# Output projection of a hybrid decoder layer: operand loads on another queue, a buffer for the sum of two weight blocks, later splits and a store in pieces

## The chip, the cores and the metric

The kernel runs on one core of a Trainium2 chip. The time is device microseconds (us) of one execution; lower is better. A core has a matrix engine (TensorE, PE in the profile), a vector engine (VectorE, DVE), a scalar engine (ScalarE, ACT), GpSimd (POOL) and SyncE (SP). Transfers between device memory and the on-chip memory are issued by SP, ACT or POOL, each strictly in the order of its own queue, and moved by 16 DMA engines.

## The reference

One decoder layer over a prompt of 1024 tokens and 8 x 8 sample tokens, with model width 2048. RMSNorm and one input projection make five groups of 1024 columns; group A goes through a short convolution and a gated linear recurrence, group B through a gate, a convolution of width 31, LayerNorm and SiLU. Both halves, `ya` and `yb`, then go through one output projection, a residual sum and a final RMSNorm:

```
proj = jnp.einsum('btd,de->bte', xn, w_in)             # input projection, split in five
...
y = jnp.einsum('bte,ed->btd', jnp.concatenate([ya, yb], axis=-1), w_out)
return x32 + y, h[:, -1], new_buf_a, new_buf_b          # then the final RMSNorm over x32 + y
```

Everything is float32.

## The kernel before, in words

**Splits.** PE multiplies numbers of reduced mantissa (float32r). So every operand is split into a high part, a cast on ACT, and a low part, the operand minus its high part on DVE. A product of two operands is three matmuls: high x high, high x low, low x high.

**The input projection** takes the first 979 us. At its end `finish_b(i)` (L687) makes, for each of the eight blocks of channels, the operands of the output projection and stores them to device memory through POOL: `d7d`, `yd`, `o2d` (L698 to L702). It needs the A half `ya`, which `load_a(i)` (L665) loads through SP (L668); the tile `ya` has one buffer, so the load waits until the store of `o2d` of block i-1, which reads that buffer, has ended. For the last block `load_a(NC - 1)` and `finish_b(NC - 1)` are called behind the last projection.

**The output projection** is done in blocks, with seven products of half-size matrices in place of eight (the list `products`, L753 on). Each product p takes rows of one stored operand (`d6d`, `o2d`, `d7d`, `yd`) and either one block of `w_out` or the sum or difference of two; its result is added to one or two quarters of the output, which start as the residual `x`. Products 0 to 6 run in that order. A product has two column halves j of 512 and eight steps k in each, 16 steps in all; a step is four token tiles x three matmuls of 128 x 512 (L852 to L854), and in products 1, 3, 4 and 5 two more for the sample tokens (L860). After the eighth step of a half DVE adds the four banks of results to `c` (L983), so that the banks come free.

**Per step.** `load_w(s)` (L806) loads one or two 256 KB weight blocks through SP (L817) into `or`; `split_out(s)` (L828) adds the two in place on DVE (L843, products 0, 2, 3, 4 and 6), casts the high part on ACT (L844) and subtracts on DVE (L845). The tile `or` is free after L845. There are eight such tiles in products 0 and 1 (they lie where the input projection's operands lay) and five after that; the split is called two steps ahead of the matmuls (`AHEAD`), and its high and low parts have three buffers.

**Operands.** `load_op(p, k)` (L771) loads one 256 KB operand block through SP (L776) and splits it at once (L777 on ACT, L778 on DVE). It is called for product p+1 at step 2k of product p; its tile is the one that step k of product p-1 used. The eight loads of product 0 are called ahead of its first step.

**Queues.** The order of instructions on an engine is the order of a planner: it simulates the engines' clocks and gives each engine, at each moment, the ready instruction of the best priority. Priority is the program's order; `tc.high_priority(URGENT)` moves instructions 200 places ahead, `tc.high_priority(-LATER)` 400 back. So an instruction can be put ahead of its place in the program where the planner finds it ready. On the chip each engine then follows that order strictly.

**The end.** The last eight steps are done one token tile at a time. For each of the four tiles the row scale comes out of `inverse` (L873), ACT scales 768 columns (L1013), DVE 1024 and 256 (L1014, L1016), and two stores of 512 KB go out on SP (L1015, L1017).

Of the kernel before, what the change touches and what calls it, by code (L numbers as in the profile page):

```python
# [7 lines left out]
F32 = mybir.dt.float32  # L8
F32R = mybir.dt.float32r
AF = mybir.ActivationFunctionType  # L10
ALU = mybir.AluOpType
# [3 lines left out]
P = 128  # L15
# [3 lines left out]
NC = W // P  # L19
# [4 lines left out]
T = SEQ + NS  # L24
# [11 lines left out]
URGENT = 200  # L36
LATER = 400
# [26 lines left out]
def hybrid_layer_kernel(  # L64
# [21 lines left out]
    nc = tc.nc  # L86
    V, S, G, PE = nc.vector, nc.scalar, nc.gpsimd, nc.tensor
# [3 lines left out]
    wp = ctx.enter_context(tc.tile_pool(name="wp", bufs=3))  # L91
# [147 lines left out]
    yd = [dp.tile([P, T], F32, name=f"yd{k}") for k in range(NK)]  # L239
# [6 lines left out]
    AHEAD = 2  # L246
# [12 lines left out]
    NH = NK // 2  # L259
# [144 lines left out]
    def tt(name, dt=F32):  # L404
        return kb.tile([P, 364], dt, tag="t", name=name, bufs=9)
# [259 lines left out]
    def load_a(i):  # L665

        ya = early[i] = kb.tile([P, AS + DB * AW], F32, tag="xa", name=f"ya{i}")
        nc.sync.dma_start(ya[:, :T], yd[i])  # L668
        if i == NC - 1:
            return  # L670
        h = G0 // 2
        for o in (0, h):
            d = tt(f"d6_{i}_{o}")[:, :h]
            V.tensor_sub(d, ya[:, G0 + o : G0 + o + h], ya[:, o : o + h])
            G.dma_start(d6d[i][:, o : o + h], d)
# [28 lines left out]
    for n in range(4 * NC, 5 * NC):  # L704
        i = n - 4 * NC
# [31 lines left out]
    H = D // 2  # L737
    NB = H // 512
    NN = G0 // P
    NH = NK // 2  # L740

    def rows(tiles, o):
        return lambda k: tiles[k][:, o : o + G0]

    def smp(tiles, o):
# [6 lines left out]
    products = [  # L752
        (rows(d6d, 0), ((0, 0), add, (0, 1)), (((1, 1), add),), None),  # L753
        (rows(o2d, 0), ((0, 0), None, None), (((1, 0), add), ((1, 1), sub)), s12),
        (rows(d7d, G0), ((0, 0), add, (1, 1)), (((0, 0), add), ((1, 1), add)), None),
        (rows(b_y, G0), ((1, 0), sub, (0, 0)), (((0, 0), add), ((1, 0), add)), s2),
        (rows(a_y, 0), ((0, 1), sub, (1, 1)), (((0, 1), add), ((1, 1), add)), s1),
        (rows(b_y, 0), ((1, 1), None, None), (((0, 0), sub), ((0, 1), add)), s12),
        (rows(d7d, 0), ((1, 0), add, (1, 1)), (((0, 0), add),), None),
    ]  # L760
# [8 lines left out]
    cq, ops, sops, osplit = {}, {}, {}, {}  # L769

    def load_op(p, k):  # L771
        b = p % 2 * NH + k
        hi = xp.tile([P, G0], F32R, tag=f"h{b}", name=f"yh{p}_{k}")
        lo = xp.tile([P, G0], F32R, tag=f"l{b}", name=f"yl{p}_{k}")
        raw = lo.bitcast(F32)
        nc.sync.dma_start(raw, products[p][0](k))  # L776
        S.copy(hi, raw)  # L777
        V.tensor_sub(lo, raw, hi.bitcast(F32))  # L778
        ops[p, k] = (hi, lo)

    def load_samples(src, name):

# [37 lines left out]
    def load_ahead(s):  # L820

        while (t := len(begun)) < last0 and t < s + (NH if steps[t][0] < 2 else 5):
            load_w(t)
            begun.append(t)
# [3 lines left out]
    def split_out(s):  # L828
        if s not in wraw:
            load_w(s)  # L830
        p, j, k = steps[s]
        _, op, wb = products[p][1]
        ra, rb = wraw.pop(s)
        if s >= last0:

            big = xp.tile([P, H], F32R, tag=held[s - last0], name=f"ow{s}")
            hi, lo = big[:, :512], big[:, 512:]
        else:
            hi = wp.tile([P, 512], F32R, tag="wh", name=f"oh{s}")
            lo = wp.tile([P, 512], F32R, tag="wl", name=f"ol{s}")  # L840
        with tc.high_priority(URGENT):
            if wb is not None:
                V.tensor_tensor(ra, ra, rb, op)  # L843
            S.copy(hi, ra)  # L844
            V.tensor_sub(lo, ra, hi.bitcast(F32))  # L845
        osplit[s] = (hi, lo)
# [83 lines left out]
    def then(p, st, f):  # L930
        between.setdefault(p * NB * NH + st, []).append(f)

    for p in range(NP - 1):
        for k in range(NH):
            then(p, 2 * k, lambda p=p, k=k: load_op(p + 1, k))
        if products[p + 1][3] is not None:
            then(p, 4, lambda p=p: load_samples(*products[p + 1][3]))

# [16 lines left out]
    for k in range(NH):  # L955
        then(5, 9 + 2 * k, lambda k=k: split_out(last0 + k))

    for k in range(NH):
        load_op(0, k)
        load_ahead(k + 1 - NH)  # L960
    for s in range(AHEAD):
        split_out(s)
    for s, (p, j, k) in enumerate(steps[:last0]):
        _, _, dests, sm = products[p]
        if k == 0:
            pts = [bank(f"po{p}_{j}_{n}") for n in range(NN + (sm is not None))]
        load_ahead(s)
        if s + AHEAD < last0:
            split_out(s + AHEAD)
        for f in between.pop(s, ()):  # L970
            f()
        for n in range(NN):
            multiply(s, n, pts[n])
        if sm is not None:
            multiply_samples(s, pts[NN])
        osplit.pop(s)
        if k < NH - 1:
            continue
        js = slice(j * 512, (j + 1) * 512)
        with tc.high_priority(URGENT):  # L980
            for n in range(NN):
                for q, op in dests:
                    V.tensor_tensor(cq[q, n][:, js], cq[q, n][:, js], pts[n], op)  # L983
        if sm is not None:
            h = shalf[p]
            z = zs[0][:NS, h * H + j * 512 : h * H + (j + 1) * 512]

            low = ob.tile([P, 512], F32, tag="sq", name=f"zl{p}_{j}", bufs=2)[:NS]
            S.copy(low, pts[NN][NS:])
            V.tensor_tensor(z, z, pts[NN][:NS], ALU.add)  # L990
            V.tensor_tensor(z, z, low, ALU.add)
        if p == NP - 1:
            for n in range(NN):
                squares_of(n * P, P, cq[(0, 0), n][:, js], 2)
                gain(cq[(0, 0), n][:, js], 0)

    for n in range(NN):
        t = n * P
        z = cq[(0, 0), n]
        widths = ((0, 512),) if n < NN - 1 else ((0, 256), (256, 256))  # L1000
        for m, (c0, cn) in enumerate(widths):
            pt = bank(f"pz{n}_{m}")
            for k in range(NH):
                multiply(last0 + k, n, pt[:, :cn], slice(c0, c0 + cn))
            zz = z[:, 512 + c0 : 512 + c0 + cn]
            V.tensor_tensor(zz, zz, pt[:, :cn], ALU.add)
            squares_of(t, P, zz, 3 + m)
            if m < len(widths) - 1:
                gain(zz, 512 + c0)
        w = inverse(t, P, 3 + len(widths), lambda: gain(zz, 512 + c0))  # L1010
        zr = cq[(0, 1), n]
        h = 256
        S.activation(zr[:, h:], zr[:, h:], AF.Copy, scale=w)  # L1013
        V.tensor_scalar(z, z, w, None, ALU.mult)  # L1014
        nc.sync.dma_start(y[t : t + P, :H], z)  # L1015
        V.tensor_scalar(zr[:, :h], zr[:, :h], w, None, ALU.mult)  # L1016
        nc.sync.dma_start(y[t : t + P, H:], zr)  # L1017


# [76 lines left out]
```

## Time and profile before

| | us |
|---|---|
| median of 3 runs | 1351.22 (1349.5 to 1356.63) |
| profiled execution, its own time | 1354.75 |
| its span | 1353.0 |
| PE busy in it | 1321.1 (98%) |
| DVE busy | 1065.5 (79%) |
| ACT busy | 551.4 (41%) |
| POOL busy | 100.1 (7%) |

The profile is one execution, which took 3.5 us more than the median. A "busy" PE is a modelled figure, since matmuls overlap in the array; PE's real rate is read from how many matmuls a stretch holds. An idle time is shown with what ended it ("<-DVE c L983": an instruction of line 983 on DVE that wrote c). SPq, POOLq and so on are the queues that issue transfers.

### The profile page before, as it was taken

The page shows a single profiled execution, that of the slowest core. Times are in us where ns is not written, and L with a number is a line of the kernel's source. Part 1 is how long each engine was busy: PE and PEld are TensorE (multiplying, and loading weights), DVE is VectorE, ACT ScalarE, POOL GpSimd, SP SyncE. Part 2 cuts the span into 40 slices and gives each one's busy share as a digit, 9 for nine tenths or more (in the row PEclk, how much of TensorE's full clock was granted, in tenths as well). Part 3 has the DMA queues.
Part 4 walks back from the last instruction along what each step waited for, and adds up shares of the span by engine and source line. Part 5 has one row for each costly group of instructions (what it writes and reads, how often), then busy time and mean ns, then how long its engine had stood idle before and what let it go on. Part 6 is the DMA issues. An engine that isn't in the chain of part 4 may idle for free.

```text
span 1353.0 us, 18432 instructions
## 1 busy us (share of the span) xinstructions
PE 1321.1 (98%) x6794; PEld 1150.0 (85%) x6794; DVE 1065.5 (79%) x1842; ACT 551.4 (41%) x891; POOL 100.1 (7%) x190
## 2 busy tenths in 40 slices
PE   9999999999999999999999999999979999989997
PEld 7888888888888888888888898888868787768876
DVE  6449979898998996997987986766565676667977
ACT  7744627217237146155164165322232332224553
POOL 0210020100100010000001000012100000000100
PEclk9999999999999999999999999999989999999998
DMA  8831141312312322223123133276799668665663
GB/s 297 309 100 44 47 78 47 76 48 68 72 46 73 61 65 63 52 68 60 45 67 67 48 105 63 80 245 226 255 319 322 240 201 271 187 189 164 226 210 140
DMA packets 85946, 180.71 MB, mean 134 GB/s; under 512 B 14176, under 2 KB 18272, under 8 KB 85600
## 3 DMA queue, kind: packets, MB, share of 16 engines
q1 hardware_dynamic: 73952, 141.63, 34.0%
q0 software_dynamic: 11760, 37.90, 10.1%
q8 instruction: 53, 0.87, 0.3%
q14 instruction: 37, 0.30, 0.1%
q10 hardware_dynamic: 144, 0.01, 0.0%
HBM read 147.31 MB, written 32.19 MB: 133 GB/s over the span
## 4 chain that ended last, share of the span: by engine, by line
PE 74%; DMA 12%; DVE 10%; issue 1%; SPq 1%; ACT 0%; DVEq 0%; POOL 0%; ACTq 0%
PE pp L230 61%; DMA or<-in_w_out_dram 7%; DVE cb L449 4%; PE po L852 3%; PE po L854 3%; PE po L853 3%; PE po L860 1%; DVE ol L845 1%; DMA yl<-yd 1%; DVE c L983 1%; DMA yl<-o2d 1%; SPq L817 1%; DMA cbd<-cb 1%; DVE wl L160 1%; DMA c<-in_x_dram 1%
## 5 line engine op out<-in xcount | busy, mean ns | idle before, releaser
L230 PE MATMUL pp<-xg,wh 128*128 128x320 f32 (+1 forms) x1920 | 461.7, 335 | 1.2 <-DVE xg L194 1.2
L230 PEld LDWEIGHTS pp<-xg,wh 128*128 128x128 f32 x1920 | 320.3, 188 | 40.8 <-DVE xg L194 2.1
L449 DVE SCALAR_TENSOR_TENSOR cb<-u,prm,cb 128x1024 f32<-128x1024 f32 x240 | 307.2, 1280 | 1.3
L230 PE MATMUL pp<-xl,wh 128*128 128x512 f32 x640 | 250.9, 392 | 0.6 <-DVE xl L194 0.6
L230 PE MATMUL pp<-xh,wh 128*128 128x512 f32 x640 | 251.1, 393 | 0.4 <-ACT xh L193 0.3
L159 ACT CAST wh<-wr 128x512 fp32r<-128x512 f32 (+1 forms) x161 | 98.7, 614 | 341.7 <-PE pp L230 276.6
L230 PE MATMUL pp<-xg,wl 128*128 128x256 f32 (+1 forms) x1280 | 196.4, 296 | 0.0
L230 PEld LDWEIGHTS pp<-xg,wl 128*128 128x128 f32 x1280 | 186.0, 189 | 0.0
L852 PE MATMUL po<-oh,yh 128*128 128x512 f32 x416 | 165.7, 398 | 13.9 <-DVE c L983 7.6
L230 PE MATMUL pp<-xh,wl 128*128 128x512 f32 x640 | 171.2, 389 | 0.0
L853 PE MATMUL po<-ol,yh 128*128 128x512 f32 x416 | 165.5, 398 | 2.3 <-DVE ol L845 2.2
L854 PE MATMUL po<-oh,yl 128*128 128x512 f32 x416 | 164.8, 396 | 0.0
L160 DVE TENSOR_TENSOR wl<-wr,wh 128x512 fp32r<-128x512 f32 (+1 forms) x161 | 109.9, 683 | 46.4 <-ACT wh L159 29.4
L230 PEld LDWEIGHTS pp<-xh,wl 128*128 128x128 f32 x640 | 120.1, 188 | 25.0
L230 PEld LDWEIGHTS pp<-xh,wh 128*128 128x128 f32 x640 | 120.7, 189 | 21.5 <-ACT xh L193 0.9
L230 PEld LDWEIGHTS pp<-xl,wh 128*128 128x128 f32 x640 | 120.6, 189 | 20.6 <-DVE xl L194 1.5
L852 PEld LDWEIGHTS po<-oh,yh 128*128 128x128 f32 x416 | 79.9, 192 | 33.2 <-DVE c L983 9.3
L843 DVE TENSOR_TENSOR or<-or 128x512 f32<-128x512 f32 x80 | 54.2, 689 | 63.9 <-DMA or<-in_w_out_dram 63.4
L853 PEld LDWEIGHTS po<-ol,yh 128*128 128x128 f32 x416 | 79.9, 192 | 21.6 <-DVE ol L845 4.9
L844 ACT CAST oh<-or 128x512 fp32r<-128x512 f32 x104 | 64.1, 618 | 78.9 <-PE po L860 50.2
L854 PEld LDWEIGHTS po<-oh,yl 128*128 128x128 f32 x416 | 79.7, 192 | 16.7
L777 ACT CAST yh<-yl 128x512 fp32r<-128x512 f32 x56 | 34.7, 620 | 127.3 <-DMA yl<-yd 59.8
(218 smaller groups left out, 1409.4 us busy)
## 6 DMA issues: line engine op xcount, KB each, us to landing
or<-in_w_out_dram SPq DMA_DIRECT2D x192, 256.0 KB, 4.4
wr<-in_w_in_dram SPq DMA_DIRECT2D x152, 256.0 KB, 3.0
xt<-in_x_dram POOLq DMA_DIRECT2D x16, 512.0 KB, 6.4
c<-in_x_dram SPq DMA_DIRECT2D x16, 512.0 KB, 6.4
xraw<-in_xT_dram SPq DMA_DIRECT2D x15, 544.0 KB, 6.2
yl<-yd SPq DMA_DIRECT2D x24, 256.0 KB, 4.6
cbd<-cb POOLq DMA_DIRECT2D x8, 544.0 KB, 5.5
yd<-sga POOLq DMA_DIRECT2D x8, 544.0 KB, 8.8
```

Source lines behind the costliest of these rows:

```text
L159: S.copy(hi[:, sl], raw[:, sl])
L160: V.tensor_sub(lo[:, sl], raw[:, sl], hi[:, sl].bitcast(F32))
L230: PE.matmul(out, w, mv, start=fl, stop=ll)
L449: V.scalar_tensor_tensor(cb[:, :SEQ], u[:, j : j + SEQ], w, cb[:, :SEQ], ALU.mult, ALU.add)
L777: S.copy(hi, raw)
L817: nc.sync.dma_start(r, w_out[r0 : r0 + P, c0 : c0 + 512])
L843: V.tensor_tensor(ra, ra, rb, op)
L844: S.copy(hi, ra)
L845: V.tensor_sub(lo, ra, hi.bitcast(F32))
L852: PE.matmul(pt, yh, hi, start=k == 0, stop=False)
L853: PE.matmul(pt, yh, lo, start=False, stop=False)
L854: PE.matmul(pt, yl, hi, start=False, stop=k == NH - 1)
```

## The change

Four things change. (1) The sum of two weight blocks goes to a tile of its own, `ws`, with two buffers, and no longer in place. (2) The operand loads of all products but product 1 go through POOL's queue instead of SP's; from product 1 on they are called at step k, not 2k; the split is a function of its own, called five steps behind step 2k, and for product 0 two steps ahead of its matmuls, with URGENT priority. (3) The last `ya` load goes through POOL, with LATER priority. (4) Each of the last four token tiles is stored in four pieces: 384 KB on ACT's queue, two of 256 KB and one of 128 KB on SP's; DVE's scaling of 1024 columns is done in two halves.

```diff
     def load_a(i):
         ya = early[i] = kb.tile([P, AS + DB * AW], F32, tag="xa", name=f"ya{i}")
+        if i == NC - 1:
+            with tc.high_priority(-LATER):
+                G.dma_start(ya[:, :T], yd[i])
+            return
         nc.sync.dma_start(ya[:, :T], yd[i])
-        if i == NC - 1:
-            return
...
     def load_op(p, k):
         hi = xp.tile([P, G0], F32R, tag=f"h{b}", name=f"yh{p}_{k}")
         lo = xp.tile([P, G0], F32R, tag=f"l{b}", name=f"yl{p}_{k}")
+        (nc.sync if p == 1 else G).dma_start(lo.bitcast(F32), products[p][0](k))
+        ops[p, k] = (hi, lo)
+
+    def split_op(p, k):
+        hi, lo = ops[p, k]
         raw = lo.bitcast(F32)
-        nc.sync.dma_start(raw, products[p][0](k))
         S.copy(hi, raw)
         V.tensor_sub(lo, raw, hi.bitcast(F32))
-        ops[p, k] = (hi, lo)
...
     def split_out(s):
             if wb is not None:
-                V.tensor_tensor(ra, ra, rb, op)
+                ws = wp.tile([P, 512], F32, tag="wr", name=f"ws{s}", bufs=2)
+                V.tensor_tensor(ws, ra, rb, op)
+                ra = ws
             S.copy(hi, ra)
             V.tensor_sub(lo, ra, hi.bitcast(F32))
...
     for p in range(NP - 1):
         for k in range(NH):
-            then(p, 2 * k, lambda p=p, k=k: load_op(p + 1, k))
+            then(p, 2 * k if p == 0 else k, lambda p=p, k=k: load_op(p + 1, k))
+            then(p, 2 * k + 5, lambda p=p, k=k: split_op(p + 1, k))
...
+    def split_first(k):
+        with tc.high_priority(URGENT):
+            split_op(0, k)
+
+    for k in range(AHEAD, NH):
+        then(0, k - AHEAD, lambda k=k: split_first(k))
     for k in range(NH):
         load_op(0, k)
         load_ahead(k + 1 - NH)
     for s in range(AHEAD):
         split_out(s)
+        split_first(s)
...
         S.activation(zr[:, h:], zr[:, h:], AF.Copy, scale=w)
-        V.tensor_scalar(z, z, w, None, ALU.mult)
-        nc.sync.dma_start(y[t : t + P, :H], z)
+        nc.scalar.dma_start(y[t : t + P, H + h :], zr[:, h:])
+        for o in (0, 512):
+            V.tensor_scalar(z[:, o : o + 512], z[:, o : o + 512], w, None, ALU.mult)
+            nc.sync.dma_start(y[t : t + P, o : o + 512], z[:, o : o + 512])
         V.tensor_scalar(zr[:, :h], zr[:, :h], w, None, ALU.mult)
-        nc.sync.dma_start(y[t : t + P, H:], zr)
+        nc.sync.dma_start(y[t : t + P, H : H + h], zr[:, :h])
```

## Rows read from the trace of the kernel before

**Rows 1.** Stretches: length, busy us (instructions) per engine, PEclk, DMA share, GB/s.

```profile
979.00:1033.30 54.30, 46.99 (x194) 37.72 (x193) 35.44 (x58) 18.18 (x31) 1.59 (x3) 0.91 0.91 306
1033.30:1086.90 53.60, 51.52 (x225) 41.81 (x224) 32.18 (x53) 18.65 (x32) 0.00 (x0) 1.00 0.78 264
1086.90:1131.80 44.90, 44.18 (x194) 35.90 (x193) 33.16 (x54) 14.79 (x26) 0.00 (x0) 1.00 0.70 216
1131.80:1189.30 57.50, 54.14 (x225) 42.78 (x224) 36.81 (x59) 14.33 (x25) 1.08 (x4) 0.97 0.73 221
1189.30:1245.60 56.30, 53.02 (x226) 43.04 (x225) 37.90 (x62) 16.34 (x28) 0.00 (x0) 0.97 0.60 182
1245.60:1296.40 50.80, 50.80 (x226) 42.07 (x225) 40.64 (x81) 25.59 (x60) 4.27 (x8) 1.00 0.65 222
1296.40:1344.30 47.90, 45.87 (x217) 38.29 (x215) 41.44 (x89) 24.02 (x59) 0.54 (x1) 0.96 0.44 150
```

**Rows 2.** Timeline of PE: start, length, instruction, [idle before it <- what ended it].

```profile
990.80 0.80 PE L852 MATMUL po<-oh,yh 128*128 128x512 f32 x1 [6.12 <-ACT oh L844]
...
1194.59 0.50 PE L852 MATMUL po<-oh,yh 128*128 128x512 f32 x1 [3.04 <-DVE c L983]
```

**Rows 3.** Chain of waits, in order of time: start, length, what.

```profile
971.14 8.73 DMA o2d<-ya
...
1187.10 4.27 DMA yl<-yd
...
1191.39 0.63 ACT yh L777
...
1192.65 0.68 DVE ol L845
1193.34 2.40 DVE c L983 x4
...
1196.80 0.43 PE po L852
```

**Rows 4.** Waits of SP's queue from 960 us: us in total, times, longest.

```profile
SPq L817 <- DVE ol L845: 127.2, 69, 5.4
...
SPq L776 <- PE po L860: 23.1, 15, 3.2
SPq L668 <- DMA o2d<-ya: 9.0, 1, 9.0
```

**Rows 5.** Timeline of SP's queue from 1060 us.

```profile
1068.09 12.53 SPq L776 DMA_DIRECT2D yl<-yd  x5
```

**Rows 6.** Line 776, the operand loads: who waited for it (us, times).

```profile
  ACT yh L777: 126.1, 50
```

**Rows 7.** Waits in the output projection.

```profile
DVE or L843 <- DMA or<-in_w_out_dram: 63.4, 41, 5.2
```

**Rows 8.** Timeline of DVE in product 2.

```profile
1108.32 0.69 DVE L843 TENSOR_TENSOR or<-or 128x512 f32<-128x512 f32 x1 [1.51 <-DMA or<-in_w_out_dram]
1108.93 0.68 DVE L845 TENSOR_TENSOR ol<-or,oh 128x512 fp32r<-128x512 f32 x1
```

**Rows 9.** Groups of POOL: busy us, mean ns, idle before.

```profile
L453 POOL DMA_DIRECT2D cbd<-cb x8 | 4.4, 548 | 27.4 <-DVE cb L449 27.4
```

**Rows 10.** The page's transfers: count, KB each, median us from issue to landing.

```profile
or<-in_w_out_dram SPq DMA_DIRECT2D x192, 256.0 KB, 4.4
...
xt<-in_x_dram POOLq DMA_DIRECT2D x16, 512.0 KB, 6.4
...
yl<-yd SPq DMA_DIRECT2D x24, 256.0 KB, 4.6
...
yd<-sga POOLq DMA_DIRECT2D x8, 544.0 KB, 8.8
```

**Rows 11.** Timeline of all engines at the end.

```profile
1346.66 0.75 DVE L1014 TENSOR_SCALAR c<-c,r 128x1024 f32<-128x1024 f32 x1
...
1347.87 0.37 SPq L1017 DMA_DIRECT2D out_y_dram<-c  x1
```

## The prediction

> **What bounds the kernel now.** I read the stretches first, cut where the seven products of the output projection begin [rows 1]. A product is 16 steps of 12 matmuls (14 where the samples ride along). The product at 1245.6 us has 16 x 14 = 224 matmuls, PE busy all through, in 50.8 us: 0.2268 us each. By that pace a product of 192 takes 43.55 us, one of 224 takes 50.8, and the last stretch (168 full matmuls and 48 of half width) 43.55. Taken from the stretches this leaves a loss of 54.3-43.55 = 10.75, then 2.8, 1.35, 6.7, 5.5, 0 and 4.35 us: **31.4 us in which PE has work left and does not do it**. That is all the change can win before the last matmul; the tail has its own term below. The projection before 979 us is not touched.
>
> Next I looked at what ended PE's waits [rows 2]. The largest is 6.1 us before step 2 of the first product, ended by a cast of ACT; five others sit where a bank of results has to be emptied and DVE (L983) comes late; the one shown waited 3.0 us. After each large one matmuls run at 0.43 us for a while [rows 3], the lower clock level, which makes a stall dearer by about 2 us. Who made ACT and DVE late is in the chain of waits [rows 3]: a 256 KB operand load of 4.27 us, the cast that waits for it, the low half of a weight step behind that cast, and only then the four evacuations PE wants. ACT and DVE are late because they work strictly in their queue's order behind a transfer. Three couplings do this:
>
> (a) SP waits. 127.2 us go on `or` loads that wait for L845 to free a raw buffer, 23.1 on operand loads that wait for PE, and 9.0 once, on the last `ya`, behind the store of `o2d` [rows 4]. Five operand loads in a row, each released by a step of PE, held SP from 1068 to 1080.6 us, and the weight loads stood behind them [rows 5].
> (b) ACT waits 126.1 us in 50 casts for operand loads [rows 6]; `oh` stands behind them.
> (c) DVE waits 63.4 us in 41 adds for weight loads [rows 7]. The add of a later step stands ahead of an older step's L845 [rows 8], while the load it needs was issued after an L845 of two steps before. So two steps must cover a load (4.4 us [rows 10]), two issues and two DVE instructions: close to 6 us against 2 x 12 x 0.2268 = 5.4 us of PE work. The ring is five deep and acts as if it were two.
>
> **The change part by part.**
>
> The sum buffer adds no instruction and no memory traffic: the add writes elsewhere. In the two-block products the raw buffer is free after the add (0.69 us long [rows 8]) instead of after add, cast and subtraction; with two sum buffers an add can't run ahead of the subtraction two steps older. The ring then gives five steps, 13.6 us, to cover about 6 us. Coupling (c) should go in products 0, 2, 3, 4 and 6. In products 1 and 5 there is no sum and the raw buffer is freed as before.
>
> The operands of six products go to POOL: 48 loads, and the last `ya`, 49 issues. At the 548 ns of a POOL issue [rows 9] that is 26.9 us on an engine that is idle in this stage; it costs nothing as long as nothing is queued behind on POOL. What is queued there: the three stores of the last `finish_b`, four tiny copies in product 3 and eight stores of finished tiles in product 5. POOL now takes the waits for PE and for `o2d`; SP is left with weights, residual blocks, sample operands and product 1's operands. Loading at step k instead of 2k asks for up to 256 KB per step in a product's first half; the DMA shares of 0.60 to 0.78 after the first product [rows 1] have room.
>
> Landing times decide whether ACT still waits. A 256 KB load through SP took 4.6 us; the trace has no such load through POOL. Bounds: 4.6, and 8.8 for a 544 KB store through POOL; a 512 KB load there took 6.4 [rows 10]. The nearest, half of 6.4's bytes, is a load: I take 5 us. The split is meant to come five steps later, 13.6 us, which covers either bound. The queue order of the casts comes from the planner's own simulated clock, however, so a cast can be put forward to where the planner thinks the load has landed. Even then ACT loses only 1 to 4 us per step, against a lead of two steps (5.4 us) less 1.3 us for `oh` and `ol`.
>
> The last `ya` moves from SP to POOL, so SP's 9.0 us go. Its own time hardly improves: the `o2d` store issued at 971.14 took 8.73 us [rows 3], so `ya` can't be issued before 979.9, plus 0.55 us on POOL, plus a flight between 4.6 and 8.8 us: it lands at 985 to 989. The add of `finish_b` that reads it (L697) will stand in DVE's order near 984 by my estimate: some 5 us of scaling, activation and multiplying behind the end of the projection, with DVE no longer late. DVE can therefore block for 1 to 5 us, against two steps already prepared. Bounds of the cost to PE: 0 and about 3 us.
>
> The last tile. Now the row scaling takes 0.75 us, then two stores are issued, the second at 1347.87 [rows 11]. In halves the first store goes some 0.25 us sooner, ACT's piece goes out beside them, and the last piece is 128 instead of 512 KB; one more DVE instruction and one more SP issue stand on the path. I take -0.3 us, with bounds -0.7 and +0.5. Tiles 0 to 2 do the same behind PE's work and cost nothing.
>
> **Sum.** What stays of each loss: product 0, 3.5 of 10.75 (the `ya` wait, and 0.91 of the DMA time in use); product 1, 1.0 of 2.8; product 2, 0.5 of 1.35; products 3 and 4, 1.5 of 6.7 and of 5.5, since eight evacuations still make DVE busy for some 5 us in a row; the last, 1.0 of 4.35. That is 9.0, so 31.4 - 9.0 + 0.3 = 22.7 us less. The profiled execution took 1354.75 us, 1353.0 of it span, and would become 1332.0; it lies 3.5 us above the median of the runs, so against the median, 1351.2 - 22.7 = **1328.5 us**. With nothing left and the best tail the median would be 1351.2 - 31.4 - 0.7 = 1319.
>
> **The rivals.**
>
> *The transfers bind in the first two products.* For: DMA shares of 0.91 and 0.78 there, 306 and 264 GB/s, and the same bytes have to come in 10 us less [rows 1]. Against: weights are taken eight steps ahead there, and part of that traffic was prefetch. Then the 13.5 us of products 0 and 1 stay and only 17.9 - 4.5 + 0.3 = 13.7 go: 1337.5 us. Beside this case stands the Trainium skill, DMA: Bandwidth & Descriptors, "Issuing engines are not separate DMA queues": loads issued by different engines share the same 16 DMA engines, and a second issuer only saves issue time. By that rule POOL brings no bandwidth; the trace has no stretch with loads of this size from both queues to set beside it.
>
> *The split doesn't move.* The planner puts each cast straight behind its load's simulated landing, as it did before, and ACT keeps its waits. For: 50 of 56 casts waited for their load [rows 6]. Then couplings (a) and (c) go and (b) stays; the stalls whose chain runs through a cast are the 6.1 us one with its slow clock (about 10 us) and those of products 3 and 4 (12 us), of which I leave half, 11, and the 9.0 of above: 31.4 - 20 + 0.3, so 1339.5 us.
>
> *No difference.* Each stall is replaced by the next late thing, DVE's evacuations above all: around 1350 us.
>
> *Slower.* One mechanism: POOL's loads land late and ACT stands in order behind them. If each of the 48 takes 8.8 instead of 4.6 us and its cast is at the old place, ACT waits 48 x 4.2 = 202 us more. Today 126.1 + 63.4 = 189.5 us of such waits [rows 6, 7] go with 31.4 us of loss, a sixth; 202 us would make 33 us, from which the freed SP and the sum buffer take about 16: 1368 us. It decides from a flight of about 4.1 us beyond the planner's landing, the lead computed above. Against: no POOL issue group is stretched; eight stores that directly followed DVE's tap instructions took 548 ns each [rows 9]. Beside it stands a rule of the Trainium skill (SBUF — State Buffer, "SBUF: two separate sides"): while VectorE holds the port pair it shares with GpSimd, in a two-port mode, GpSimd can't write descriptors, and such a load belongs on a hardware queue. By that rule flights would stretch as in this rival; rows 9 don't bear it out so far.
>
> **How the numbers follow.** Forecast 0.58 (its own range 1320 to 1336), transfers bind 0.15, split doesn't move 0.11, no difference 0.08, slower 0.08. A measurement of this kernel tells about 0.5% from no change, 6.8 us: the first three cases are faster, 0.84. From 1320 (nearly everything won) up to 1347 (the two partial cases with some microseconds more left) about 8 in 10 lie inside.
>
> **What would show it.** Right: no SP wait on `o2d`; the SP waits on L845 gone but for products 1 and 5; DVE waits on `or` in a few places only; PE without a gap above 3 us after 979 and at full clock in all products. Wrong in a step: casts still waiting for `yl` by 100 us or more; a DVE wait on `ya` near 985; DMA shares above 0.95 in product 0 with PE waiting on `or`. Wrong altogether: PE's loss unchanged, or new gaps that end at a POOL load.

## The result and the profile after the change

The kernel after takes 1342.62 us (median of four runs, 1341.06 to 1344.0) against 1352.51 us (four runs, 1349.5 to 1356.63) for the kernel before: a ratio of 0.992, 95% interval 0.9896 to 0.9943. It is faster by 9.9 us, where 22.7 were forecast; the range held the time, the size did not hold. The profiled execution took 1342.78 us (span 1341.1), 12.0 us less than that of before. Of this the stretches give 12.4.

Stretches of the kernel after, cut where its seven products begin; columns as in [rows 1]:

```profile
979.36:1035.85 56.49, 48.91 (x194) 36.62 (x193) 35.60 (x57) 19.74 (x34) 5.94 (x11) 0.97 0.96 334
1035.85:1086.92 51.07, 51.06 (x225) 41.97 (x224) 28.25 (x46) 15.38 (x28) 4.30 (x8) 1.00 0.68 222
1086.92:1131.74 44.82, 44.10 (x194) 35.96 (x192) 35.13 (x57) 15.32 (x27) 4.30 (x8) 1.00 0.74 236
1131.74:1182.60 50.86, 50.86 (x226) 41.96 (x224) 37.58 (x61) 14.94 (x26) 5.39 (x12) 1.00 0.79 253
1182.60:1233.48 50.88, 50.88 (x226) 41.97 (x224) 37.31 (x61) 15.15 (x26) 4.30 (x8) 1.00 0.53 169
1233.48:1284.25 50.77, 50.77 (x225) 42.04 (x224) 39.62 (x79) 24.88 (x59) 4.81 (x9) 1.00 0.68 227
1284.25:1332.19 47.94, 45.10 (x217) 36.84 (x215) 42.51 (x91) 24.28 (x59) 0.54 (x1) 1.00 0.42 139
```

Taken as in the prediction (43.55 or 50.8 us of work per stretch), the losses are 12.9, 0.3, 1.3, 0.1, 0.1, 0 and 4.4: 19.0 us against 31.4 [rows 1]. Products 3 and 4 lost 12.2 us and now lose almost nothing. Of that, 5.4 us was PE's busy time, which fell from 54.14 and 53.02 to 50.86 and 50.88, while the granted clock went from 0.97 to 1.00 of the 2.4 GHz level. The clock is only a part of these 5.4 us: 0.03 of stretches of 57.5 and 56.3 us make 3.4 us, an estimate. Busy time also grows without it, since matmuls overlap in the model: in run 1 below, product 3 shows 52.53 us at a clock of 1.00. Product 0 is worse by 2.2 us, and the last stretch is where it was.

Who waited in the output projection of the kernel after (us, times, longest); the first five answer to [rows 6, 7], the sixth to the wait for `o2d` in [rows 4]:

```profile
DVE ws L851 <- DMA or<-in_w_out_dram: 14.2, 7, 4.2
ACT yh L784 <- DMA yl<-yd: 49.0, 23, 5.5
ACT yh L784 <- DMA yl<-d7d: 24.7, 13, 3.8
ACT yh L784 <- DMA yl<-o2d: 21.0, 8, 5.1
ACT yh L784 <- DMA yl<-d6d: 8.1, 1, 8.1
POOL ya L670 <- DMA o2d<-ya: 7.8, 1, 7.8
```

DVE's wait for weights fell from 63.4 to 14.2 us. ACT's casts still wait 102.8 us for their operands (126.1 before): the split that the code puts five steps later was not moved (the first cast for product 1 ran at 987.14 us, in step 1 of product 0, where the code puts it at step 5). SP now waits in its queue from 960 us on like this, `ws` being the add that frees the raw buffer:

```profile
SPq L823 <- DVE ws L851: 111.8, 45, 18.4
SPq L823 <- DVE ol L854: 52.2, 23, 8.0
```

These waits are longer than before (164.0 us against 127.2), yet DVE waits less for weights: SP now waits because its buffers are full ahead of need, up to 18.4 us at a time.

### The profile page after: what moved, and what is told of

It is laid out like the page before. It is cut to its first block, busy times and chain, and to the rows that moved or that the text cites. A ratio compares the mean times of both kernels' runs of the same rounds, so it can differ in the third digit from the quotient of the medians.

```text
span 1341.1 us, 18459 instructions
## 1 busy us (share of the span) xinstructions
PE 1316.5 (98%) x6794; PEld 1145.5 (85%) x6794; DVE 1066.1 (79%) x1846; ACT 551.2 (41%) x891; POOL 128.2 (10%) x239
## 3 DMA queue, kind: packets, MB, share of 16 engines
q0 software_dynamic: 15744, 51.04, 12.9%
## 4 chain that ended last, share of the span: by engine, by line
PE 76%; DVE 12%; DMA 5%; issue 4%; POOL 1%; ACT 1%; SPq 0%; DVEq 0%; POOLq 0%; ACTq 0%
PE pp L230 59%; DVE cb L449 5%; PE po L862 5%; PE po L863 4%; PE po L861 4%; DMA or<-in_w_out_dram 3%; PE po L869 2%; DVE wl L160 1%; DMA cbd<-cb 1%; DMA yl<-d7d 1%; DVE cb L450 1%; DVE c L905 1%; DVE xc L500 1%; DMA yl<-o2d 1%; DVE c L1001 0%
## 5 line engine op out<-in xcount | busy, mean ns | idle before, releaser
L785 DVE TENSOR_TENSOR yl<-yl,yh 128x512 fp32r<-128x512 f32 x56 | 38.3, 689 | 50.7 <-ACT yh L784 50.7
L450 DVE SCALAR_TENSOR_TENSOR cb<-u,prm,cb 128x64 f32<-128x64 f32 x240 | 69.2, 288 | 4.3
```

Source lines behind the costliest of these rows:

```text
L450: V.scalar_tensor_tensor(cs, us[:, :, j : j + DS], w, cs, ALU.mult, ALU.add)
```

## The experiments

Losses of TensorE by product (us, taken from each kernel's own stretches as above), and the comparison with the kernel before. A sum belongs to the profiled execution alone, a median to two to ten executions (run 9 has one). The profiled executions of runs 6 and 11 took 1343.0 and 1339.7 us, 3.2 above and 3.5 below their medians. The kernel before was measured again beside each group of runs (medians 1352.1 to 1354.7), so runs of different groups are compared by their ratios.

| kernel | 0 | 1 | 2 | 3 and 4 | 5 | last | sum | median us | ratio (95%) |
|---|---|---|---|---|---|---|---|---|---|
| before | 10.8 | 2.8 | 1.4 | 12.2 | 0 | 4.4 | 31.4 | 1352.5 | |
| after | 12.9 | 0.3 | 1.3 | 0.1 | 0 | 4.4 | 19.0 | 1342.6 | 0.992 (0.9896 to 0.9943) |
| 1 no sum buffer | 13.5 | 2.4 | 2.6 | 11.1 | 0 | 4.3 | 33.8 | 1355.6 | 1.0015 (1.0002 to 1.0028) |
| 2 sum buffer alone | 8.6 | 0.2 | 0 | 1.6 | 0 | 6.5 | 16.9 | 1340.9 | 0.9905 (0.9884 to 0.9926) |
| 3 loads on POOL alone | 11.0 | 0.8 | 3.5 | 10.1 | 0 | 4.3 | 29.6 | 1355.5 | 1.0023 (1.0004 to 1.0041) |
| 4 sum buffer, `ya` on POOL | 6.4 | 0.5 | 0 | 1.6 | 0 | 8.0 | 16.5 | 1338.7 | 0.9901 (0.9887 to 0.9916) |
| 5 sum buffer, all loads on POOL | 12.7 | 0.8 | 0.9 | 0.4 | 0 | 4.4 | 19.1 | 1344.1 | 0.9937 (0.992 to 0.9953) |
| 6 after, operands on SP | 7.1 | 1.4 | 0 | 2.3 | 0 | 8.8 | 19.4 | 1339.8 | 0.9904 (0.9883 to 0.9925) |
| 7 after, product 2 on SP | 7.3 | 1.0 | 0.8 | 2.6 | 0 | 5.2 | 16.9 | 1341.2 | 0.9922 (0.9897 to 0.9948) |
| 8 after, casts tied | 8.9 | 4.1 | 0 | 0 | 0 | 6.0 | 18.9 | 1341.7 | 0.9903 (0.9881 to 0.9925) |
| 9 as 8, half the weights in product 0 | 8.6 | 2.2 | 0 | 0 | 0 | 7.0 | 17.6 | 1340.2 | one run |
| 10 as 8, sample casts tied | 0 | 12.2 | 0 | 0 | 0 | 5.5 | 17.6 | 1342.0 | 0.9921 (0.9897 to 0.9945) |
| 11 as 10, early loads held back | 0 | 9.8 | 0 | 0 | 0 | 5.4 | 15.1 | 1343.3 | 0.991 (0.9883 to 0.9936) |
| 12 after, last weights early | 12.1 | 0.7 | 0.3 | 1.6 | 4.1 | 0.5 | 19.3 | 1343.9 | 0.9926 (0.9912 to 0.9941) |
| 13 as 4, product 5 packed | 7.0 | 0 | 0 | 1.9 | 0.6 | 0.5 | 9.8 | 1333.5 | 0.9869 (0.9852 to 0.9886) |
| 14 as 13, `o2d` first | 5.5 | 0 | 0 | 3.1 | 0.8 | 0.5 | 9.8 | 1335.0 | 0.9867 (0.985 to 0.9884) |

### Which part gains: runs 1 to 3

Run 1 is the kernel after with the sum back in place:

```diff
-                ws = wp.tile([P, 512], F32, tag="wr", name=f"ws{s}", bufs=2)
-                V.tensor_tensor(ws, ra, rb, op)
-                ra = ws
+                V.tensor_tensor(ra, ra, rb, op)
```

> The changed kernel with the sum in place again, everything else as changed. If the sum buffer is what freed the ring of weight buffers, the losses of products 2, 3 and 4 come back towards 1.3, 6.7 and 5.5 us and the time goes to 1350 or more; if the operand loads on POOL did that, they stay below 1.5 us each and the time near 1343.

Run 2 is the kernel before with these three lines in place of that one, and nothing else.

> The kernel before with the sum buffer alone. If the sum buffer is what freed the ring, products 2, 3 and 4 lose below 4 us together in place of 13.5 and the time is 1340 to 1344; if the loads on POOL are needed, they keep 9 us or more and the time is 1348 to 1353.

Run 3 is the kernel before with the loads moved:

```diff
-        nc.sync.dma_start(raw, products[p][0](k))
+        (nc.sync if p == 1 else G).dma_start(raw, products[p][0](k))
...
-            then(p, 2 * k, lambda p=p, k=k: load_op(p + 1, k))
+            then(p, 2 * k if p == 0 else k, lambda p=p, k=k: load_op(p + 1, k))
```

together with `load_a`'s part of the change (the last `ya` on GpSimd's queue).

> The kernel before with one part of the change: operand loads of six products and the last ya through GpSimd's queue, at step k; the split stays right behind the load, the sum stays in place, the last tile is as before. Theory 1 (only the sum buffer gains): products 2 to 4 keep about 13 us of loss, DVE waits for raw weights stay above 55 us, the time is 1351 to 1357 us. Theory 2 (the freed SP queue gains as well, and the late split or the last tile gave it back in the version without the sum buffer): 1345 us or less, with SP's 9 us wait for o2d gone from the losses of the first product.

The three agree. The sum buffer alone gives the whole gain, 1340.9 us, and without it the rest is worth nothing: both runs with the sum in place come out 0.15 to 0.23% slower, with intervals just above 1. DVE's waits for raw weights, in run 1, run 3 and run 2:

```profile
DVE or L849 <- DMA or<-in_w_out_dram: 67.2, 43, 6.0
```
```profile
DVE or L845 <- DMA or<-in_w_out_dram: 62.8, 40, 3.5
```
```profile
DVE ws L844 <- DMA or<-in_w_out_dram: 12.7, 6, 3.8
```

They stay where they were [rows 7] as long as the add writes into its own raw buffer, whatever SP is freed of. Run 2's products 2 to 4:

```profile
1081.21:1124.73 43.52, 43.52 (x193) 36.05 (x192) 32.46 (x52) 13.62 (x23) 0.00 (x0) 1.00 0.71 228
1124.73:1177.18 52.45, 51.46 (x225) 41.82 (x224) 39.04 (x65) 16.45 (x29) 1.09 (x4) 1.00 0.77 244
1177.18:1227.95 50.77, 50.77 (x225) 42.04 (x224) 37.69 (x62) 16.01 (x27) 0.00 (x0) 1.00 0.58 178
```

### What the moved loads cost: runs 4 to 7

Run 4 adds to run 2 only `load_a`'s part. Run 5 is run 3 with the sum buffer. Run 6 is the kernel after with one line changed, run 7 with the same line changed for product 2 alone:

```diff
-        (nc.sync if p == 1 else G).dma_start(lo.bitcast(F32), products[p][0](k))
+        nc.sync.dma_start(lo.bitcast(F32), products[p][0](k))
...
+        (nc.sync if p in (1, 2) else G).dma_start(lo.bitcast(F32), products[p][0](k))
```

> The kernel before with the sum buffer and, besides it, only the last ya through GpSimd's queue; operands stay on SP. In the sum-buffer-only run SP stood 7.8 us behind ya's wait for o2d while the transfers ran at a share of 0.39, and the first product lost 8.6 us. Theory 1 (that hold is what delays the casts of the first product): the loss of the first product falls to 3 to 5 us and the time to about 1336. Theory 2 (the transfers of 965 to 1000 us bind, whichever queue they are in): the loss of the first product stays at 8 to 11 us, the time at 1339 to 1342.

> Sum buffer, operands and last ya through GpSimd's queue at step k, but the split right behind the load and the last tile as before. Theory 1 (the operand loads on GpSimd's queue are what the first product of the changed kernel pays for: they run ahead of need and stand behind the three stores of the last block): loss of the first product 10 to 13 us, time 1340 to 1344. Theory 2 (the urgent, early casts of product 0's operands are the cost, the queue is not): loss of the first product 6 to 8.6 us as with the operands on SP, time 1337 to 1340.

> The changed kernel with the operand loads back on SP's queue and all else as changed: sum buffer, split five steps behind the load, product 0's operands cast urgently, ya on GpSimd's queue, last tile in four pieces. Theory 1 (the queue costs): the loss of the first product falls from 12.9 to 6 to 8.6 us, the time is 1336 to 1340. Theory 2 (the early casts cost): it stays at 10 to 13 us, the time at 1340 to 1344. By either, products 2 to 4 lose under 3 us together.

> The changed kernel with one difference: product 2's eight operand loads stay on SP's queue, as product 1's do. Theory 1 (on GpSimd's queue they run ahead into steps 12 to 15 of the first product, and their casts stand ahead of that product's weight casts): the loss of steps 12 to 15 of the first product falls from 4.1 to under 1 us, that of its steps 0 to 3 stays at 7 to 9 and that of the last stretch at about 4, so the time falls by 3 to 4 us, to about 1339. Theory 2 (any operand load on GpSimd's queue costs there): steps 12 to 15 still lose 3 to 4 us, the time is 1341 to 1344.

Run 4 against run 5 is the move of the operand loads, that is, GpSimd's queue together with the call at step k in place of 2k: 1338.7 and 1344.1 us, intervals apart, so the two cost some 5 us. Their place is product 0 (6.4 and 12.7 us). The queue by itself is what runs 6 and 7 change: run 6, with all else as in the kernel after, loses 7.1 us there where the kernel after loses 12.9, but its time is not apart from that of the kernel after. By groups of four steps the kernel after loses 8.5, 0, 0.4 and 4.1 us, run 6 loses 5.7, 0, 0.7 and 0.7, and run 7 loses 7.3, 0, 0 and 0.

How the last four steps lose is plain in the trace. GpSimd's queue (first lines) and ACT (second) in the kernel after:

```profile
1012.79 0.55 POOL L778 DMA_DIRECT2D yl<-d7d  x1 [13.22 <-PE po L863]
1015.51 0.54 POOL L778 DMA_DIRECT2D yl<-d7d  x1 [2.17 <-PE po L863]
```
```profile
1027.64 0.62 ACT L784 CAST yh<-yl 128x512 fp32r<-128x512 f32 x1 [3.80 <-DMA yl<-d7d]
1028.16 0.61 ACT L853 CAST oh<-ws 128x512 fp32r<-128x512 f32 x1
1031.18 0.62 ACT L784 CAST yh<-yl 128x512 fp32r<-128x512 f32 x1 [2.41 <-DMA yl<-d7d]
1031.71 0.62 ACT L853 CAST oh<-ws 128x512 fp32r<-128x512 f32 x1
```

and what it did to PE:

```profile
1028.83 0.49 PE L861 MATMUL po<-oh,yh 128*128 128x512 f32 x1 [1.11 <-ACT oh L853]
1029.63 0.50 PE L862 MATMUL po<-ol,yh 128*128 128x512 f32 x1 [0.31 <-DVE ol L854]
```

The `d7d` rows are product 2's operands. The code places their loads at product 1's first steps (from 1035.85) and their splits five steps behind. On GpSimd's empty queue the first went out at 1012.79, as soon as PE's step had freed an operand buffer, and the planner put the casts there too, each ahead of a weight cast that PE needed next. On SP, behind the weight loads, most of them can't go out that early: in run 7 two of the eight did before product 1 began. The transfers from 960 to 1036 us (count, KB, median us from issue to landing), kernel before and kernel after:

```profile
or<-in_w_out_dram SPq DMA_DIRECT2D x41, 256.0 KB, 5.9
...
yl<-d7d SPq DMA_DIRECT2D x1, 256.0 KB, 11.7
```
```profile
or<-in_w_out_dram SPq DMA_DIRECT2D x40, 256.0 KB, 8.5
...
yl<-d7d POOLq DMA_DIRECT2D x7, 256.0 KB, 7.3
```

The first four steps of the kernel after lose by the same order, but for older loads. Product 0's first seven operand loads were out by 964.5 us; the eighth went out on GpSimd's queue directly behind three stores of `finish_b`, and its cast stood in ACT's order ahead of a weight cast:

```profile
972.10 0.55 POOL L704 DMA_DIRECT2D o2d<-ya  x1
972.64 0.55 POOL L778 DMA_DIRECT2D yl<-d6d  x1
```
```profile
981.76 0.62 ACT L784 CAST yh<-yl 128x512 fp32r<-128x512 f32 x1 [8.10 <-DMA yl<-d6d]
982.28 0.61 ACT L853 CAST oh<-ws 128x512 fp32r<-128x512 f32 x1
987.14 0.62 ACT L784 CAST yh<-yl 128x512 fp32r<-128x512 f32 x1 [4.24 <-DMA yl<-o2d]
```

This stall is not new: the same four steps lost 10.7 us in the kernel before, the last four 0.1. What the place behind the stores costs by itself, no run separates.

Run 7 shows the mechanism of the last four steps: with product 2's loads on SP the last four steps lose nothing, as theory 1 said. The time it gave fell short all the same: products 3 and 4 lost 2.5 us more than in the kernel after, and 1341.2 us is not measurably below 1342.6. In run 6 likewise the last stretch took back what product 0 gave (8.8 us for 4.4), in an execution slower than its median, and its interval overlaps that of the kernel after. In these profiles what is gained in one stage is in part lost in the next, and only the pair of runs 4 and 5 is apart by measurement.

Run 4 also gives `ya`'s part alone: steps 0 to 3 of product 0 lose 5.5 us where run 2 loses 8.6. The sums keep 0.5 us of that, and the medians, 1338.7 and 1340.9, point the same way, with overlapping intervals. Product 0's 6.4 us and the time lie between the ranges of the two theories. (The share of 0.39 in the expectation holds for the end of SP's wait alone; from 970 to 978 us run 2's transfers ran at 0.82.)

### Order of the casts, or transfers: runs 8 to 11

In run 8 each operand cast is put behind the last weight cast that precedes it in the program:

```diff
+            anchor[0] = S.copy(hi, ra)
-            S.copy(hi, ra)
...
+        with tc.issue_after(anchor[0].ins):
+            S.copy(hi, raw)
-        S.copy(hi, raw)
```

> The changed kernel with one edit: each operand cast on ACT is queued behind the weight cast that the program has just called, so the planner can't put it forward; loads and transfers stay. Theory A (the first product loses 12.9 us because casts for later products stand in ACT's order ahead of weight casts and wait for loads with flights of 7 to 10 us): the first product's loss falls below 4 us, ACT's waits for operand loads from 103 to below 30 us, the time to 1332 to 1336 us. Rival B (the 16 DMA engines are full from 966 to 1002 us and the weights come late in whatever order): the loss stays at 10 us or more, with PE's waits now ending at adds that wait for weight loads; time 1341 to 1344 us.

In run 9, in product 0, the second block's load is dropped and the add is `ra + ra`.

> The changed kernel with the casts tied behind the weight casts, as in the run with tied casts, and in the first product only the first of the two weight blocks is loaded (2 x 256 KB becomes 256 KB per step) and added to itself, so the first product computes with twice one block in place of the sum. Theory 1 (transfers bind in the first two products): their loss, 8.9 + 4.1 us in the run with tied casts, falls below 4 together, and the time by 8 us or more, to about 1332. Theory 2 (the order of ACT's queue binds, and the bytes do not): the loss of the first two products stays above 10 us, the time within 3 us of the tied run.

Steps 0 to 3, which lost 8.5 us, now lose 0.0 in both, and no operand cast waits for its load in either. Steps 12 to 15, which lost 4.1, lose 0.0 too, although product 2's loads still went out early (in run 8 from 1004.75 us on). So both stalls were made by order: a cast that waits for its load, ahead of an older weight. Yet run 8 stalled in steps 8 to 11, for a cast that was not tied, that of the samples:

```profile
1015.32 0.62 ACT L799 CAST s<-s12r 128x512 fp32r<-128x512 f32 x1 [9.99 <-DMA s12r<-o2d]
```
```profile
1016.51 0.80 PE L863 MATMUL po<-oh,yh 128*128 128x512 f32 x1 [5.47 <-ACT oh L855]
```

With 8.9 us lost in product 0, run 8 fits neither theory A (below 4) nor rival B (10 or more); its time is rival B's. Run 9 had the same stall with fewer weight bytes (10.8 us in the first two products), but its transfers were at a share of 0.97 to 1.05 from 967 to 1011 us all the same: other early loads filled the room. It says nothing on what the bytes cost. Run 10 ties the sample cast too and moves it from step 4 to step 14. Run 11 also holds back what is not needed yet:

```diff
             then(p, 4, lambda p=p: load_samples(*products[p + 1][3]))
+            then(p, 14, lambda p=p: split_samples(*products[p + 1][3]))
...
-        (nc.sync if p == 1 else G).dma_start(lo.bitcast(F32), products[p][0](k))
+        with tc.issue_after(anchor[1].ins) if p == 2 else nullcontext():
+            (nc.sync if p in (1, 2) else G).dma_start(lo.bitcast(F32), products[p][0](k))
...
+    then(2, 9, load_gain)
```

(`anchor[1]` is the last weight load; the loads of the residual blocks (1, 0) and of the gain are tied in the same way.)

> The changed kernel with the operand casts tied behind the weight casts of their step, as in the first run with tied casts, and besides the cast of the sample operands moved from step 4 to step 14 of the product and tied as well. In the first tied run steps 0 to 3 of the first product lost 0.0 us in place of 8.5, and steps 8 to 11 lost 8.9 behind the sample cast, which waited 10.0 us for its loads. Theory 1 (the first product loses by casts that stand in ACT's order ahead of an older weight cast, the transfers themselves would suffice): its loss falls from 8.9 to under 2 us, the time by 6 to 8 us against the tied run, to 1333 to 1336. Theory 2 (the transfers bind, the stall only moves to the next cast): the first two products together still lose 9 us or more, the time stays at 1339 to 1344.

> The run with operand and sample casts tied lost 0.0 us in product 0 and 12.2 us in product 1, in one stall behind 256 KB loads with flights of up to 15 us. Here, besides the tied casts, loads that are not needed yet are held back: product 2's operands go through SP behind the weight load of their step, the residual blocks of (1, 0) are tied behind a weight load of product 1, and the 1 MB gain is loaded in product 2 instead of product 0. Theory 1 (what binds in the first two products is transfers taken ahead of need): the first two products lose under 4 us together, the time is 1331 to 1335. Theory 2 (the bytes that the two products need bind by themselves): they lose 8 us or more, the time is 1338 to 1343.

In both, product 0 loses nothing: 16 steps at full pace, in run 10 at transfer shares of 1.03 and 1.05 from 990 to 1010 us. The forecast's 3.5 us were not out of reach for that product. But the loss came back in product 1, in one stall each, as theory 2 of run 10 said (12.2 us, 1342.0). Chain of waits of run 10 (start, length, what), and its stall:

```profile
1016.42 7.25 DMA or<-in_w_out_dram
...
1023.68 14.96 DMA c<-in_x_dram
...
1038.72 6.55 DMA or<-in_w_out_dram
```
```profile
1046.03 0.79 PE L873 MATMUL po<-ol,yh 128*128 128x512 f32 x1 [9.29 <-DVE ol L865]
```

The load of 14.96 us is a 512 KB residual block, not one of 256 KB as the expectation of run 11 has it. Run 11, without those loads in the way, still has one, of 7.47 us at 1032.16, behind weight loads of 9.87 and 4.73 us. By its numbers theory 2 holds: the loss is 9.8, and the median, 1343.3 us, lies at the upper end of its range. Yet it is not shown that the bytes are the cause, and one row speaks against it: the mean share fell to 0.70 from 1010 to 1020 us, just ahead of the stall, with 8 sample loads of 32 KB holding SP for 5.14 us. What sets the floor of the first two products (5.5 us in the best run, 9.8 with everything tied and held) stays open.

### The last stretch: runs 12 to 14

Chain of waits of the kernel after, and DVE there:

```profile
1271.58 4.91 DMA or<-in_w_out_dram
...
1278.69 5.81 DMA or<-in_w_out_dram
...
1284.62 0.70 DVE ws L851
```
```profile
1284.62 0.69 DVE L851 TENSOR_TENSOR ws<-or 128x512 f32<-128x512 f32 x1 [4.17 <-DMA or<-in_w_out_dram]
...
1287.94 2.47 DVE L1001 TENSOR_TENSOR c<-c,po 128x512 f32<-128x512 f32 x4
```

These are the weights of the last eight steps. They are loaded when they are split, and not ahead; each takes a buffer of the ring of five when the one before is done with. DVE stands 4.17 us in an add for one of them, and the evacuations that PE waits for stand behind it (PE's wait of 2.82 us at 1289.27 ends with one). Run 12 loads them four steps earlier:

```diff
+        then(5, 5 + 2 * k, lambda k=k: load_w(last0 + k))
         then(5, 9 + 2 * k, lambda k=k: split_out(last0 + k))
```

> The changed kernel with one edit: the loads of the last eight weights are called four steps before their split, not together with it. Theory C (the last stretch loses 4.1 us, as before the change, because DVE stands 3 to 4 us in an add for a weight that was loaded only when its split was called): the loss falls below 1.5 us, time 1339 to 1341. Rival D (four banks with eight adds of DVE at the end of product 5 are the cause): the loss stays near 4 us and the time at 1342.6.

The loss moved from the last stretch to product 5 (4.1 us; a gap at 1264.96 behind a DVE that waited 2.45 us for the same loads): five buffers look too few for both uses. Theory C's loss came (0.5 us in the last stretch), its time did not (1343.9). Run 13 starts from run 4 and makes room instead:

```diff
-            raw = ob.tile([P, H], F32, tag="wr2", name=f"or{s}", bufs=5)
+            raw = pair.pop() if pair else ob.tile([P, H], F32, tag="wr2", name=f"or{s}", bufs=5)
...
+        if p == 5 and k % 2 == 0:
+            pair.append(raw)
+        elif p == 5:
+            ra, rb = rb, ra
...
+        then(5, 7 + 2 * k, lambda k=k: load_w(last0 + k))
```

> As the run with sum buffer and last ya alone on GpSimd's queue, and besides: product 5, which needs one block of weights per step, puts two steps into one raw buffer, and the last eight weights are loaded two steps before their split. Theory 1 (the last stretch loses because its weights find no free raw buffer and are loaded on demand): the loss of products 5 and 6 together falls from about 6 to 2 us or less, 4 us below the run without packing. Theory 2 (the eight last casts and the squares of finished tiles keep ACT and DVE too busy there): the loss stays at 4 to 6 us.

Theory 1 held: products 5 and 6 lose 1.0 us in place of 8.0, and the time fell by 5.2 us. DVE's wait for weights from 1225 us on:

```profile
DVE ws L851 <- DMA or<-in_w_out_dram: 0.9, 2, 0.6
```

At 1333.5 us run 13 beats the kernel after (0.9869, interval 0.9852 to 0.9886, against 0.992) with the operands on SP, the split and the last tile as before, and the packing as a new part. In run 14 `finish_b` stores `o2d` ahead of its two larger blocks (in all eight calls, not in the last alone):

> The run with sum buffer, last ya on GpSimd's queue and packed weights, and besides: the last block's o2d store, for which ya waits, goes out ahead of its two larger stores. Theory 1 (what is left in the first product, 7.0 us, is transfers in the wrong order, 0.5 MB stores ahead of data that a cast waits for): ya is issued some 3 us sooner and the loss of the first product falls to 3 to 5 us, the time to 1329 to 1331. Theory 2 (the sum of the bytes between 965 and 1000 us binds, not their order): the loss stays at 6 to 8 us, the time at 1332 to 1335.

`ya` went out at 975.74 instead of 978.72 and product 0 lost 5.5 instead of 7.0 us, but product 3 lost more (3.1 against 1.9). The loss lies between the two theories, the time with theory 2; no difference from run 13 by time. Run 10 with run 13's packing, and run 11 with it, were also run:

> The same, and besides two steps of product 5 in one raw buffer and the last eight weights loaded two steps before their split, as in the packed run. Theory 1: losses of the first product under 2 us and of the last stretch under 1 us add up, the time is 1326 to 1331. Theory 2: the first two products lose 9 us or more, only the last stretch gains, the time is 1334 to 1339.

> The same, and besides two steps of product 5 in one raw buffer and the last eight weights loaded two steps before their split. Theory 1: the first two products lose under 4 us and products 5 and 6 under 5, the time is 1327 to 1332. Theory 2: the first two products lose 8 us or more, the time is 1335 to 1342.

They took 1341.8 us (0.9914, 0.9891 to 0.9938) and 1339.6 us (0.9888, 0.9861 to 0.9916), with 14.0 and 10.5 us lost in the first two products and 6.4 and 4.8 in the last two. Product 1's stall was there again, and on top of tied casts the packing gained less than in run 13: the last two products had lost 5.5 and 5.4 us without it. For the first of the two that is a miss, since theory 2 gave it 1334 to 1339 us.

## Why the prediction was wrong in its size

**The base and the ceiling** held: losses and spans of the two profiles agree (12.4 of 12.0 us). The forecast was made against a median of 1351.2, the comparison has 1352.5 and 1342.6, so 9.9 us are left of a difference of 12.0 between the profiles, and 2.1 of the missing 12.8 us lie there. Ten more are the losses (19.0 where 9.0 were to stay), the rest tail and start.

**Sum buffer** (the coupling through the ring, "five deep acts as two"): right, and larger than said. It was to leave 0.5 and 1.5 and 1.5 us in products 2, 3 and 4. It left 1.3, 0.1 and 0.1: nothing gained in product 2, nearly all in products 3 and 4. Run 2 shows that no other part was needed.

**"What stays of each loss", product 0: 3.5 us.** This is the step that failed most: 12.9 us stayed, 9.4 more than forecast. Two things make it up: 8.5 us in steps 0 to 3, where 10.7 had been lost before, so that most of the old stall stayed; and 4.1 us in steps 12 to 15, which are new. The wait of DVE for `ya`, for which the 3.5 us stood in part, did not come. The prediction reasoned from the freed SP; what it freed was early transfers. It counted 256 KB more per step "in a product's first half" against the shares after the first product, and did not ask when GpSimd's queue would really issue them. The prediction itself had the two halves of the cause among its rivals. "The transfers bind": 13.5 us were to stay in the first two products and 13.2 did. Runs 10 and 11 show product 0 without a loss, but 12.2 and 9.8 us in the two products together, so this rival is weakened and not excluded. Its sign came by half: the share was 0.96, above 0.95, but from 975 to 1036 us no add of DVE waited for weights. "The split doesn't move": ACT's waits stayed at 102.8 us, above its own mark of 100. Neither was given the consequence seen here, that loads without a queue ahead of them run early, and take their casts with them ahead of older ones. With the operand and sample casts tied, product 0 loses nothing (shown in runs 10 and 11); that the bill then comes in product 1 is shown as well, what sets its size is not. The prediction's own sign of being right, no gap of PE above 3 us after 979, was met all the same (the longest was 2.82): many short waits made the loss.

**The last stretch: 1.0 us.** It was named beside products 2 to 4 without a reason of its own, and measured 4.4, unchanged. The wait there is for weights loaded on demand, which run 13 removed, and not for a buffer that the sum holds.

**Operands through GpSimd.** "It costs nothing as long as nothing is queued behind on POOL" was wrong by some 5 us (runs 4 and 5, which also differ in the step of the call), by the way of product 0. A load of product 0 did stand behind stores there, those of the block before the last. Their landing was no cause in the later products: 3.9 us for the 24 loads `yl<-yd` on the page, where 5 were assumed and 4.6 had been read on SP [rows 10].

**The last `ya`**: SP's 9.0 us [rows 4] went as said, and GpSimd bears 7.8. What it costs or gains in the kernel after is not to be separated there; without the operands on GpSimd steps 0 to 3 gain about 3 us by it, the whole profile 0.5 (run 4 against run 2), and the medians don't tell the two apart.

**The last tile: -0.3 us.** From the start of the last matmul to the end of the span it took 9.02 us before and 9.18 after. Over all profiles the seven kernels with the old tail took 8.62 to 9.06 (mean 8.92), the eleven with the new one 8.59 to 9.20 (mean 8.74). The difference of the means, 0.18, is smaller than the spread in either group, so the estimate is neither shown nor refuted. In the kernel after, the scalings and the four issues:

```profile
1335.05 0.88 DVE L1034 TENSOR_SCALAR c<-c,r 128x512 f32<-128x512 f32 x2
1335.56 0.81 SPq L1035 DMA_DIRECT2D out_y_dram<-c  x2
1335.85 0.35 DVE L1036 TENSOR_SCALAR c<-c,r 128x256 f32<-128x256 f32 x1
1336.01 0.35 ACTq L1032 DMA_DIRECT2D out_y_dram<-c  x1
1336.46 0.40 SPq L1037 DMA_DIRECT2D out_y_dram<-c  x1
```

The first store leaves 0.5 us after its scaling began, the last 1.4 us; before, the second and last left 1.2 us after it [rows 11].

**The rules weighed.** The slower rival did not come: the time fell, and ACT waits less for operands than before. The Trainium skill's SBUF — State Buffer, "SBUF: two separate sides", says that GpSimd can't write descriptors while VectorE holds the shared ports; no run here shows it, at 3.9 us per load beside 28 to 43 us of DVE work per product. The Trainium skill's DMA: Bandwidth & Descriptors, "Issuing engines are not separate DMA queues", says that a second issuer brings no bandwidth. The runs agree: from 979 to 990 us the kernel after moved 394 GB/s and run 6, with the operands on SP, 396.

## What to carry to other kernels

Ask of every ring when a buffer is really given back: a sum written into its own operand keeps the buffer through the whole split, and two buffers for the sum were worth all that was gained here. Loads moved to an idle queue don't only get out of the way, they run ahead, and where a planner orders an engine's work by its own clock, the work that waits for them runs ahead too and blocks what is older; look at what issue times become, not only at what the old queue is freed of. And a loss in a stretch has its own chain: the last stretch looked like the others, and its loads were simply not issued ahead.

## What the runs showed of the hardware

A stall can cost again through the clock: in products 3 and 4 of the kernel before the granted clock was 0.97, an estimate of 3.4 of the 12.2 us lost there, while in run 1 product 3 lost 6.4 us at 1.00. Near a share of 1, more early loads brought 11% more bytes and longer flights: a 256 KB weight load took 5.9 us (median of 41, at 300 GB/s) before and 8.5 us (median of 40, at 333 GB/s) after, between 960 and 1036 us. Size says little there: eight loads of 32 KB took 6.6 us in the median, about as much as the 256 KB operand loads beside them (7.3).
